# Self attention seven steps earlier, weighted values in three passes, and right factors made from the residual

## The chip, the cores and the metric

The kernel runs on one core of a Trainium2 chip. The metric is the device time of one execution in microseconds (us). Before the change the median of three runs is 722.4 us (722.18 to 723.12). The engines are called as the profile calls them: PE (TensorE, matrix products), DVE (VectorE), ACT (ScalarE), POOL (GpSimd) and SP (SyncE, which only issues transfers).

## The reference

One decoder block on 512 tokens of width 1024, in float32: gated mix of a causal pooling branch and a causal differential attention (4 heads), then cross attention to 256 memory tokens (4 heads), then a squared-ReLU MLP of width 4096, each behind an RMS norm, with residual adds, and a last RMS norm.

```python
h = rms_norm(x, g_mix)
u, q, k, v, gate_logits = split(h @ w_in)
q = apply_rope(q); k = apply_rope(k)
o = diff_attention(q, k, v, lam)     # softmax(q0 k0) - lam * softmax(q1 k1), times v, causal
y_attn = rms_norm(o, g_subln) * (1.0 - lam_init)
mixed = concat([y_pool, y_attn]) * sigmoid(gate_logits)
x = x + mixed @ w_out
x = x + memory_cross_attention(rms_norm(x, g_cross), rms_norm(mem, g_mem), w_cq, w_ckv, w_co)
x = x + square(relu(rms_norm(x, g_mlp) @ w_up)) @ w_down
return rms_norm(x, g_final)
```

## The kernel before

Everything is kept transposed: a tile holds 128 features by 512 tokens. Each float32 operand is split into a high half (`hi`, cast to fp32r by ACT, line 111) and a low half (`lo`, the difference, made by DVE, line 112), and a product is three matmuls: hi·hi, hi·lo, lo·hi (lines 105 to 107). Weights come as blocks of 128x1024; SP issues their load, ACT casts `whi`, DVE makes `wlo`, two projections ahead of their use, with three buffers of each. The split of a product's result into halves is what the next product waits for.

PE's order is written out by hand: it runs its instructions exactly as the program issues them. The orders of the other engines come from a scheduler, which takes the instructions by their dependencies and priority; `tc.high_priority()` raises the priority of what is issued inside. `tile_mm` (a projection of one 128-feature tile) runs over eight k-tiles of its input; each k-tile is a *step* of three matmuls, after which a counter ticks. `after(n, fn)` puts `fn` n steps later, so attention work is dropped between the steps of the projections.

The projections of the first stage run in the order of `PLAN`: `k0 q0 q1 k1 q2 q3 ...`, where g is a gate, u an input of the pooling branch. `qk_proj` makes a rotated q or k: after the matmuls, ACT copies the product into a quarter-swapped tile in four pieces (line 417), DVE multiplies by the cosine (418), POOL by the sine and adds (419, 420), ACT casts the two high halves (423, 425) and DVE makes the two low halves (424, 426). For k, SP copies the result into a partner-swapped tile z by two transfers (430, 431). So the tile `s` of a head holds high and low halves of both components in one array.

Twenty steps (`START`) after q0 the first attention block is due, and one more each six steps (`SPACE`): `scores(h, i)` for head h and block i of 128 queries. For each of two components c it makes two matmuls into a PSUM tile `sc` of three buffers (442, 443); DVE adds the mask and takes the maximum (445), ACT exponentiates (447); then DVE inverts the sums (449, 450), ACT scales one component (451) and DVE combines the two (452). 15 steps (`SOFTMAX`) after the scores `flip(h, i)` transposes the result on PE (463) and splits it into `at` hi and lo. Three steps after a head's last flip `attend(h)` multiplies by v into the tile `av`, over four key blocks of 512, 384, 256 and 128 columns: per block v hi times `at` hi (105), v hi times `at` lo (106), v lo times `at` hi (107). Six steps later `finish` normalises with a sum over features on PE.

In the cross attention, `cross_scores(h)` makes two `sc` tiles (in each, two query blocks), and DVE takes the maxima (684), ACT exponentiates (688), DVE normalises (692); `cross_transpose(h)` transposes and splits into `at`, and `cross_out(h)` multiplies by the memory values and splits into `xg`. The end of this stage is written as: `cross_out(0)`, `cross_scores(3)`, `cross_transpose(2)`, `cross_out(1)`, `cross_out(2)`, then the transpose and output of head 3 inside the following projection ("co").

The MLP's up projection is a Strassen-like product of 256x256 token halves A and B: left factors are sums of weight blocks, right factors sums of the weighted residual `x` (features m and m+4, halves A and B). `done_co(m)` adds the residual (line 572), makes the factors (`right_factors`, 764 to 776; the last two m at high priority) and adds the square to `ss2` (260, 261). For m below 4, x is written as a float32 tile by ACT, x(B) is replaced by the difference, and both are split in one 512-wide cast and subtraction into B11 and T1. For m of 4 and more x is written, then T2 and T3 (into `y`), then B21, B22 and T4 (`right_rest`, 790). The first MLP block (A11) uses B11 of k = 0 to 3 in that order; 11 steps after the last "co" tile PE sums `ss2` over features (234, 235).

Of the kernel before, what the change touches and what calls it, by code (L numbers as in the profile page):

```python
# [13 lines left out]
AF = mybir.ActivationFunctionType  # L14
ALU = mybir.AluOpType
AX = mybir.AxisListType

P = 128
T = 512
D = 1024  # L20
KC = D // P
NT = T // P
M = 256
# [5 lines left out]
LAM_INIT = 0.8 - 0.6 * math.exp(-0.3 * 0)  # L29
WINDOWS = (2, 4, 8, 16)  # L30
PAD = 16
START, SPACE, SOFTMAX, ATTEND, FINISH, POOLING = 20, 6, 15, 3, 6, 23
MEMIN, EARLY, LATE = 16, [4, 5, 6, 0, 1], [2, 7, 3]
WARM = 8
ON_POOL = (1, 3, 5, 7), (1, 3, 5)
# [2 lines left out]
PARTS = "A11", "A12", "A21", "A22"  # L38
ORDER = "A11", "A12", "s1", "s2", "s3", "A22", "s4"
FIRST_ORDER = "A11", "s1", "A12", "s2", "s3", "A22", "s4"  # L40
PLAN = "k0 q0 q1 k1 q2 q3 g4 k2 g5 g6 k3 g7 u0 u1 u2 u3 g0 g1 g2 g3"

G_MIX, G_CROSS, G_MEM, G_MLP, G_FINAL, PSCALE, GSUB, LAMS = 0, 8, 16, 24, 32, 40, 44, 45
NG_COL = LAMS
# [6 lines left out]
def block_kernel(ctx: ExitStack, tc: tile.TileContext, x0g, xT, memT, wv, wm, wst, wckv, wpool, vecs, csts, outT):  # L51
    nc = tc.nc
# [27 lines left out]
    def tmp(dt=F32):  # L80
        return sb("tmp", [P, T], 10, dt)
# [22 lines left out]
    def mm3(o, lh, ll, rh, rl, start, stop):  # L104
        nc.tensor.matmul(o, lh, rh, start=start, stop=False)  # L105
        nc.tensor.matmul(o, lh, rl, start=False, stop=False)  # L106
        nc.tensor.matmul(o, ll, rh, start=False, stop=stop)  # L107


    def split(hi, lo, src, eng=V):  # L110
        S.copy(hi, src)  # L111
        eng.tensor_tensor(lo, src, f(hi), op=ALU.subtract)  # L112
# [150 lines left out]
    def scaled(hi, lo, src, g):  # L263
        S.activation(hi, src, AF.Copy, scale=g)
        V.scalar_tensor_tensor(lo, src, g, f(hi), op0=ALU.mult, op1=ALU.subtract)
# [24 lines left out]
    def tile_mm(o, w, rhs, ks=range(KC), first=True, last=True):  # L290
        ks = list(ks)
        for n, k in enumerate(ks):
            c = slice(k * P, (k + 1) * P)
            mm3(o, w[0][:, c], w[1][:, c], rhs[k][0], rhs[k][1],
                first and n == 0, last and n == len(ks) - 1)
            tick()
# [31 lines left out]
    def W(*key):  # L328
        return weights(where[key])
# [82 lines left out]
    def qk_proj(which, h):  # L412
        o = acc()
        tile_mm(o, W(which, h), xg)
        a, b = tmp(), tmp()
        for j in range(4):
            S.copy(b[32 * (j ^ 1):32 * (j ^ 1) + 32, :], o[32 * j:32 * j + 32, :])  # L417
        V.tensor_tensor(a, o, cos_r, op=ALU.mult)
        ROPE_E.tensor_tensor(b, b, sin_r, op=ALU.mult)
        nc.gpsimd.tensor_tensor(a, a, b, op=ALU.add)  # L420
        s = pair("s", 6)
        top, bot = slice(0, 64), slice(64, 128)
        S.copy(s[top, 0, :], a[top, :])
        V.tensor_tensor(s[bot, 0, :], a[top, :], f(s[top, 0, :]), op=ALU.subtract)
        S.copy(s[bot, 1, :], a[bot, :])
        V.tensor_tensor(s[top, 1, :], a[bot, :], f(s[bot, 1, :]), op=ALU.subtract)
        st[which, h] = s
        if which == "k":
            z = pair("s", 6)
            nc.sync.dma_start(f(z[top, :, :]), f(s[bot, :, :]))  # L430
            nc.sync.dma_start(f(z[bot, :, :]), f(s[top, :, :]))
            st["z", h] = z
# [36 lines left out]
    def attend(h):  # L469
        at = st["at", h]  # L470
        o = ps("av", 1)
        e = slice(h * P, (h + 1) * P)
        for b in range(NT):
            vh, vl = st["v"][b]
            mm3(o[:, b * P:], vh[:, e], vl[:, e], at[0][:, b, b * P:], at[1][:, b, b * P:],
                b == 0, b == NT - 1)
        sq = tmp()
        S.activation(sq, o, AF.Square)
        sp = split_sq(sq, T)

        def finish():
            s = ps("tr", 2)
            bcast_sum(s, *sp)
            y = tmp()
            rsqrt(y, s, 1.0 / P, sq, tmp(),
                  lambda r: V.scalar_tensor_tensor(r, o, st["gsub"], r, op0=ALU.mult, op1=ALU.mult))
            merge(4 + h, y)

        after(FINISH, finish)
# [183 lines left out]
    def cross_scores(h):  # L673
        es = []
        for j in range(NT // 2):
            o = ps("sc", 3)
            for b in range(2):
                i = 2 * j + b
                tb = slice(i * P, (i + 1) * P)
                for c in range(2):  # L680
                    q, k = st["cq", 2 * h + c], st["mk", 2 * h + c]
                    mm3(o[:, b * M:(b + 1) * M], q[0][:, tb], q[1][:, tb], k[0], k[1], c == 0, c == 1)
            mx, sm = small(2), small(2)
            V.tensor_reduce(mx, o.rearrange("p (b m) -> p b m", b=2), axis=AX.X, op=ALU.max, negate=True)
            e = tmp()
            for b in range(2):
                c = slice(b * M, (b + 1) * M)
                S.activation(e[:, c], o[:, c], AF.Exp, bias=mx[:, b:b + 1], accum_out=sm[:, b:b + 1])
            V.reciprocal(sm, sm)
            for b in range(2):  # L690
                c = slice(b * M, (b + 1) * M)
                V.tensor_scalar(e[:, c], e[:, c], sm[:, b:b + 1], None, op0=ALU.mult)
            es.append(e)
        st["p", h] = es

    def cross_transpose(h):
        t = sb("at", [P, NT, T], 2, F32R)
        pt = (t[:, :MT, :], t[:, MT:, :])
        for j, e in enumerate(st["p", h]):
            tr = ps("tr", 2)  # L700
            for c in range(MT):
                for b in range(2):
                    nc.tensor.transpose(tr[:, (2 * c + b) * P:(2 * c + b + 1) * P],
                                        e[:, b * M + c * P:b * M + (c + 1) * P], ident)
            src = tr.rearrange("p (c t) -> p c t", c=MT)
            split(pt[0][:, :, j * M:(j + 1) * M], pt[1][:, :, j * M:(j + 1) * M], src)
        st["pt", h] = pt

    def cross_out(h):
        pt = st["pt", h]  # L710
        for dc in range(2):
            o = acc()
            m = 2 * h + dc
            c = slice((m % 4) * P, (m % 4) * P + P)
            for i in range(MT):
                vh, vl = st["mv", m // 4, i]
                mm3(o, vh[:, c], vl[:, c], pt[0][:, i, :], pt[1][:, i, :], i == 0, i == MT - 1)
            pr = pair("xg", 8)
            split(pr[:, 0, :], pr[:, 1, :], o)
            cross_o[m] = (pr[:, 0, :], pr[:, 1, :])  # L720
# [16 lines left out]
            after(2, cross_transpose, m // 2 - 1)  # L737
    flush()
    cross_out(0)
    cross_scores(3)  # L740
    cross_transpose(2)
    cross_out(1)
    cross_out(2)
    after(2, cross_transpose, 3)
# [11 lines left out]
    def right_factors(m, t):  # L756

        k = m % 4
        g = vec[:, G_MLP + m:G_MLP + m + 1]
        x = tmp()  # L760
        pr = pair("mix", 8)
        if m < 4:
            b12 = tmp()[:, :M]
            S.activation(x[:, A], t[:, A], AF.Copy, scale=g)
            S.activation(b12, t[:, B], AF.Copy, scale=g)
            V.tensor_tensor(x[:, B], x[:, A], b12, op=ALU.subtract)
            xs[k] = (x[:, B], b12)
            split(pr[:, 0, :], pr[:, 1, :], x)
            parts("B11", k, pr[:, 0, :], pr[:, 1, :], A)
            parts("T1", k, pr[:, 0, :], pr[:, 1, :], B)  # L770
            return
        S.activation(x, t, AF.Copy, scale=g)
        t1, b12 = xs[k]
        y = tmp()
        V.scalar_tensor_tensor(y[:, A], x[:, B], -1.0, t1, op0=ALU.mult, op1=ALU.subtract)
        V.tensor_tensor(y[:, B], x[:, B], b12, op=ALU.subtract)
        p2 = pair("s", 6)
        split(p2[:, 0, :], p2[:, 1, :], y)
        parts("T2", k, p2[:, 0, :], p2[:, 1, :], A)
        parts("T3", k, p2[:, 0, :], p2[:, 1, :], B)  # L780
        parts("B21", k, pr[:, 0, :], pr[:, 1, :], A)
        parts("B22", k, pr[:, 0, :], pr[:, 1, :], B)
        if m < KC - 1:
            right_rest(k, x, y, pr)
        else:
            rest.append((k, x, y, pr))

    def right_rest(k, x, y, pr):
        split(pr[:, 0, :], pr[:, 1, :], x)
        V.scalar_tensor_tensor(y[:, A], y[:, A], -1.0, x[:, A], op0=ALU.mult, op1=ALU.subtract)  # L790
        if k % 2 == 0:
            half["T4"] = pair("s", 6)
        c = slice(k % 2 * M, k % 2 * M + M)
        split(half["T4"][:, 0, c], half["T4"][:, 1, c], y[:, A])
        parts("T4", k, half["T4"][:, 0, :], half["T4"][:, 1, :], c)
# [10 lines left out]
    def renew():  # L806
# [2 lines left out]
        early.close()  # L809
        late["pool"] = ctx.enter_context(tc.tile_pool(name="late", bufs=1))  # L810

    projection("co", cross_o, [0, 1, 2, 3, 4, 5], [6, 7], done_co, renew, CO_ORDER)
    with tc.high_priority():
        sp2 = split_sq(ss2, T)
# [215 lines left out]
```

## Time and profile before

| | before |
|---|---|
| median of 3 runs | 722.4 us (722.18 to 723.12) |
| the profiled execution's own time | 722.57 us |
| its span, first to last instruction | 720.8 us |
| mean granted TensorE clock | 0.998 |
| busy share PE / DVE / ACT / POOL | 98% / 71% / 54% / 9% |
| DMA | 91.09 MB, mean 126 GB/s |

A row of the timeline gives the start in us, the duration, the engine, the line, the operation, output<-input and the count; in brackets stand the idle time ahead of it and what ended it. Several equal instructions in a row are one row with a count. Ends of matmuls are modelled, so neighbours overlap in the rows: a matmul of 512 columns starts 0.23 us after the last one and is shown with 0.39. A row of the window view gives a stretch and, for PE, weight loads, DVE, ACT and POOL, busy time and instructions, then granted clock, DMA share and GB/s.

### The profile page before, as it was taken

Reading aid. Unit: us, or ns where it says so; the run is one execution under the profiler, and the core shown is the slowest. Engines: PE = TensorE matmul, PEld = TensorE weight load, DVE = VectorE, ACT = ScalarE, POOL = GpSimd, SP = SyncE. Lnnn points to the kernel's source line nnn. Section 1 sums busy time; section 2 is a strip of 40 time slices with the busy share of each in tenths; the row PEclk is TensorE's granted clock in tenths of the full one; section 3 lists DMA queues with packets and bytes.
Section 4 is the critical chain, followed back from the end, with each engine's and each line's share of the span. In section 5 each row is a group of like instructions: output and inputs, shape, how many; then the busy total and the mean of one; then the engine's idle time right before and its main releaser. Section 6 shows DMA issues by size and latency. Waiting matters only on the chain.

```text
span 720.8 us, 10378 instructions
## 1 busy us (share of the span) xinstructions
PE 706.5 (98%) x4016; PEld 617.0 (86%) x4016; DVE 510.6 (71%) x797; ACT 392.5 (54%) x646; POOL 66.9 (9%) x59
## 2 busy tenths in 40 slices
PE   8999999999999999999999999999999999999995
PEld 6887888788889888888879988999889988899894
DVE  7698999975888546572999954598446973589525
ACT  7498998676766434452865641355214641256432
POOL 0044112534000000000000000000000000000000
PEclk9999999999999999999999999999999999999999
DMA  8443223143525552113924850558216661305103
GB/s 315 151 118 116 88 75 116 60 146 119 176 88 176 181 170 83 65 58 143 246 79 127 237 164 30 150 111 294 89 33 167 205 182 58 88 30 161 45 1 116
DMA packets 28257, 91.09 MB, mean 126 GB/s; under 512 B 3089, under 2 KB 5137, under 8 KB 28209
## 3 DMA queue, kind: packets, MB, share of 16 engines
q1 hardware_dynamic: 25856, 81.92, 33.5%
q0 software_dynamic: 2352, 8.52, 7.0%
q8 instruction: 31, 0.51, 0.3%
q14 instruction: 18, 0.14, 0.1%
HBM read 86.24 MB, written 2.10 MB: 123 GB/s over the span
## 4 chain that ended last, share of the span: by engine, by line
PE 89%; DVE 5%; ACT 4%; issue 1%; DMA 0%; POOL 0%; DVEq 0%; SPq 0%; ACTq 0%
PE acc L105 17%; PE acc L106 17%; PE acc L107 17%; PE sc L105 11%; PE sc L106 11%; PE sc L107 11%; ACT tmp L447 1%; PE sc L386 1%; PE sc L388 1%; PE sc L390 1%; DVE tmp L445 1%; DVE wlo L112 1%; ACT tmp L417 1%; ACT whi L111 1%; DMA wraw<-wv 0%
## 5 line engine op out<-in xcount | busy, mean ns | idle before, releaser
L111 ACT CAST whi<-wraw 128x1024 fp32r<-128x1024 f32 (+1 forms) x94 | 97.2, 1035 | 107.5 <-PE acc L106 41.0
L105 PE MATMUL acc<-xg,whi 128*128 128x512 f32 x392 | 155.0, 395 | 0.0
L107 PE MATMUL acc<-xg,wlo 128*128 128x512 f32 x392 | 153.0, 390 | 0.0
L106 PE MATMUL acc<-xg,whi 128*128 128x512 f32 x392 | 152.7, 390 | 0.0
L112 DVE TENSOR_TENSOR wlo<-wraw,whi 128x1024 fp32r<-128x1024 f32 (+1 forms) x94 | 115.1, 1226 | 26.8 <-ACT whi L111 26.4
L107 PEld LDWEIGHTS acc<-xg,wlo 128*128 128x128 f32 x392 | 73.6, 188 | 15.8
L105 PEld LDWEIGHTS acc<-xg,whi 128*128 128x128 f32 x392 | 73.7, 188 | 14.5
L106 PEld LDWEIGHTS acc<-xg,whi 128*128 128x128 f32 x392 | 73.7, 188 | 14.3
L572 DVE TENSOR_TENSOR vr<-acc,vr 128x512 f32<-128x512 f32 x39 | 26.9, 690 | 76.5 <-PE acc L107 76.4
L105 PE MATMUL sc<-mix,whi 128*128 128x256 f32 (+1 forms) x184 | 54.2, 295 | 0.0
L107 PE MATMUL sc<-mix,wlo 128*128 128x256 f32 (+1 forms) x184 | 54.1, 294 | 0.0
L106 PE MATMUL sc<-mix,whi 128*128 128x256 f32 (+1 forms) x184 | 54.0, 294 | 0.0
L164 POOL DMA_DIRECT2D mraw<-wst x16 | 13.8, 864 | 429.1 <-DMA mraw<-wst 302.3
L111 ACT CAST whi<-mraw 128x1024 fp32r<-128x1024 f32 x24 | 25.0, 1052 | 45.9 <-PE acc L106 33.0
L890 DVE TENSOR_TENSOR tmp<-sc,tmp 128x512 f32<-128x512 f32 x56 | 37.5, 684 | 6.5 <-PE sc L107 6.4
L111 ACT CAST mhl<-wraw 128x1024 fp32r<-128x1024 f32 x19 | 20.0, 1052 | 34.4 <-PE acc L106 18.0
L106 PE MATMUL acc<-xg,mhl 128*128 128x512 f32 x96 | 37.4, 390 | 0.0
L105 PE MATMUL acc<-xg,mhl 128*128 128x512 f32 x96 | 37.4, 389 | 0.0
L107 PE MATMUL acc<-xg,mhl 128*128 128x512 f32 x96 | 37.4, 389 | 0.0
L107 PEld LDWEIGHTS sc<-mix,wlo 128*128 128x128 f32 x184 | 34.5, 188 | 1.1
L105 PEld LDWEIGHTS sc<-mix,whi 128*128 128x128 f32 x184 | 34.6, 188 | 1.0
L106 PEld LDWEIGHTS sc<-mix,whi 128*128 128x128 f32 x184 | 34.5, 187 | 1.1
(274 smaller groups left out, 1731.4 us busy)
## 6 DMA issues: line engine op xcount, KB each, us to landing
wraw<-wm SPq DMA_DIRECT2D x76, 512.0 KB, 3.5
mraw<-wst SPq DMA_DIRECT2D x24, 512.0 KB, 3.9
wraw<-wckv SPq DMA_DIRECT2D x16, 512.0 KB, 3.4
mraw<-wst POOLq DMA_DIRECT2D x16, 512.0 KB, 6.1
wraw<-wst SPq DMA_DIRECT2D x16, 512.0 KB, 3.4
s<-s SPq DMA_DIRECT2D x8, 256.0 KB, 3.7
vr<-xT SPq DMA_DIRECT2D x8, 256.0 KB, 4.5
outT<-mix SPq DMA_DIRECT2D x8, 256.0 KB, 2.4
```

The lines of the kernel that those rows point to most:

```text
L105: nc.tensor.matmul(o, lh, rh, start=start, stop=False)
L106: nc.tensor.matmul(o, lh, rl, start=False, stop=False)
L107: nc.tensor.matmul(o, ll, rh, start=False, stop=stop)
L111: S.copy(hi, src)
L112: eng.tensor_tensor(lo, src, f(hi), op=ALU.subtract)
L164: nc.gpsimd.dma_start(r, part(n, then), accum_op=ALU.add)
L386: nc.tensor.matmul(o[i], xg[k][0][:, tb], wh[:, c], start=k == 0, stop=False)
L388: nc.tensor.matmul(o[i], xg[k][1][:, tb], wh[:, c], start=False, stop=False)
L390: nc.tensor.matmul(o[i], xg[k][0][:, tb], wl[:, c], start=False, stop=k == KC - 1)
L417: S.copy(b[32 * (j ^ 1):32 * (j ^ 1) + 32, :], o[32 * j:32 * j + 32, :])
L572: V.tensor_tensor(t, o, t, op=ALU.add)
L890: V.tensor_tensor(u[new], o, u[old], op=ALU.add)
```

## The change

There are five parts. `START` is 13 instead of 20 and the gates g4 and g6 stand behind k2 and k3 in `PLAN`. The rotation of q and k is a function of its own, at high priority for head 0. `attend` runs over the four key blocks in three passes instead of block by block. `cross_transpose(2)` stands ahead of `cross_scores(3)`. And `right_factors` makes all factors from the residual tile `t` with the weight g, or its negative in the small tile `ng`, inside the DVE instruction, so that the copy x is not written for m of 4 and more, and for m below 4 the halves A and B are split apart.

```diff
-START, SPACE, SOFTMAX, ATTEND, FINISH, POOLING = 20, 6, 15, 3, 6, 23
+START, SPACE, SOFTMAX, ATTEND, FINISH, POOLING = 13, 6, 15, 3, 6, 23
-PLAN = "k0 q0 q1 k1 q2 q3 g4 k2 g5 g6 k3 g7 u0 u1 u2 u3 g0 g1 g2 g3"
+PLAN = "k0 q0 q1 k1 q2 q3 k2 g4 g5 k3 g6 g7 u0 u1 u2 u3 g0 g1 g2 g3"
@@ qk_proj
         tile_mm(o, W(which, h), xg)
+        with tc.high_priority() if h == 0 else nullcontext():
+            rotate(which, h, o)
+
+    def rotate(which, h, o):
         a, b = tmp(), tmp()
...
@@ attend
-        for b in range(NT):
-            vh, vl = st["v"][b]
-            mm3(o[:, b * P:], vh[:, e], vl[:, e], at[0][:, b, b * P:], at[1][:, b, b * P:],
-                b == 0, b == NT - 1)
+        for v, a in ((0, 0), (1, 0), (0, 1)):
+            for b in range(NT):
+                nc.tensor.matmul(o[:, b * P:], st["v"][b][v][:, e], at[a][:, b, b * P:],
+                                 start=v + a + b == 0, stop=a == 1 and b == NT - 1)
@@ cross attention
     cross_out(0)
+    cross_transpose(2)
     cross_scores(3)
-    cross_transpose(2)
     cross_out(1)
@@ right_factors
-        g = vec[:, G_MLP + m:G_MLP + m + 1]
-        x = tmp()
+        g, ng = vec[:, G_MLP + m:G_MLP + m + 1], st["ng"][:, m:m + 1]
         pr = pair("mix", 8)
         if m < 4:
-            b12 = tmp()[:, :M]
-            S.activation(x[:, A], t[:, A], AF.Copy, scale=g)
+            scaled(pr[:, 0, A], pr[:, 1, A], t[:, A], g)
+            x = tmp()
+            t1, b12 = x[:, A], x[:, B]
             S.activation(b12, t[:, B], AF.Copy, scale=g)
-            V.tensor_tensor(x[:, B], x[:, A], b12, op=ALU.subtract)
-            xs[k] = (x[:, B], b12)
-            split(pr[:, 0, :], pr[:, 1, :], x)
+            V.scalar_tensor_tensor(t1, t[:, A], g, b12, op0=ALU.mult, op1=ALU.subtract)
+            xs[k] = (t1, b12)
+            split(pr[:, 0, B], pr[:, 1, B], t1)
...
-        S.activation(x, t, AF.Copy, scale=g)
         t1, b12 = xs[k]
         y = tmp()
-        V.scalar_tensor_tensor(y[:, A], x[:, B], -1.0, t1, op0=ALU.mult, op1=ALU.subtract)
-        V.tensor_tensor(y[:, B], x[:, B], b12, op=ALU.subtract)
+        V.scalar_tensor_tensor(y[:, A], t[:, B], ng, t1, op0=ALU.mult, op1=ALU.subtract)
+        V.scalar_tensor_tensor(y[:, B], t[:, B], g, b12, op0=ALU.mult, op1=ALU.subtract)
...
-    def right_rest(k, x, y, pr):
-        split(pr[:, 0, :], pr[:, 1, :], x)
-        V.scalar_tensor_tensor(y[:, A], y[:, A], -1.0, x[:, A], op0=ALU.mult, op1=ALU.subtract)
+    def right_rest(k, t, g, ng, y, pr):
+        scaled(pr[:, 0, :], pr[:, 1, :], t, g)
+        V.scalar_tensor_tensor(y[:, A], t[:, A], ng, y[:, A], op0=ALU.mult, op1=ALU.subtract)
...
+    st["ng"] = home[:, 568:568 + KC]
+    V.tensor_scalar(st["ng"], vec[:, G_MLP:G_MLP + KC], -1.0, None, op0=ALU.mult)
```

`scaled(hi, lo, src, g)`, which was there before, is an ACT copy with scale g into `hi` (line 264) and one DVE instruction src·g − hi into `lo` (265).

On PE, the rows around scores(0,0) before. `acc_541` is the projection q2, `s_395` is k0, `s_400` its swapped copy z0, `s_443` is q0, and the two `sc` tiles are the two components:

```order
L107 MATMUL acc_541<-xg_172,wlo_452 128x512
L105 MATMUL acc_541<-xg_190,whi_451 128x512
L106 MATMUL acc_541<-xg_190,whi_451 128x512
L107 MATMUL acc_541<-xg_190,wlo_452 128x512
L442 MATMUL sc_561<-s_395,s_443 128x128
L443 MATMUL sc_561<-s_400,s_443 128x128
L442 MATMUL sc_568<-s_395,s_443 128x128
L443 MATMUL sc_568<-s_400,s_443 128x128
L105 MATMUL acc_541<-xg_214,whi_451 128x512
```

And after; `acc_493` is the projection k1, which comes ahead of q2:

```order
L106 MATMUL acc_493<-xg_214,whi_406 128x512
L107 MATMUL acc_493<-xg_214,wlo_407 128x512
L446 MATMUL sc_516<-s_395,s_443 128x128
L447 MATMUL sc_516<-s_400,s_443 128x128
L446 MATMUL sc_523<-s_395,s_443 128x128
L447 MATMUL sc_523<-s_400,s_443 128x128
L105 MATMUL acc_493<-xg_232,whi_406 128x512
L106 MATMUL acc_493<-xg_232,whi_406 128x512
```

The four matmuls moved from the fourth step of q2 to behind the fifth step of k1, seven steps earlier. From here on, four is added to the line numbers.

On DVE, the rows that make k0's and q0's low halves, before (`acc_448` is q1's product):

```order
L426 TENSOR_TENSOR s_395<-tmp_386,s_395 64x512
L112 TENSOR_TENSOR wlo_497<-wraw_449,whi_496 128x1024
L418 TENSOR_TENSOR tmp_479<-acc_448,cst_68 128x512
L424 TENSOR_TENSOR s_443<-tmp_434,s_443 64x512
L426 TENSOR_TENSOR s_443<-tmp_434,s_443 64x512
L112 TENSOR_TENSOR wlo_545<-wraw_494,whi_544 128x1024
L418 TENSOR_TENSOR tmp_524<-acc_493,cst_68 128x512
```

and after:

```order
L430 TENSOR_TENSOR s_395<-tmp_386,s_395 64x512
L112 TENSOR_TENSOR wlo_497<-wraw_449,whi_496 128x1024
L422 TENSOR_TENSOR tmp_479<-acc_448,cst_68 128x512
L428 TENSOR_TENSOR s_443<-tmp_434,s_443 64x512
L430 TENSOR_TENSOR s_443<-tmp_434,s_443 64x512
L449 ISA tmp_519,small_520<-sc_516,cst_68 128x128
L449 ISA small_520 128x1
L449 ISA tmp_526,small_527<-sc_523,cst_68 128x128
```

Up to q0's second low half the order is the same; behind it the maxima of scores(0,0) took the place of the next weight's low half and of k1's product. It is the same on ACT: the order is unchanged up to q0's casts, and then the exponential of scores(0,0) stands ahead of the weight cast.

On DVE after the change, ahead of scores(3,2) (`acc_1315` is the projection u1, `sc_1332` the first component of scores(3,1), whose PSUM buffer scores(3,2) takes next):

```order
L112 TENSOR_TENSOR at_1175<-tr_1359,at_1174 128x4x128
L536 TENSOR_TENSOR padu_1372<-acc_1315,rstd_315 128x512
L535 MEMSET padu_1499 128x16
L112 TENSOR_TENSOR wlo_1393<-wraw_1316,whi_1392 128x1024
L449 ISA tmp_1335,small_1336<-sc_1332,cst_68 128x256
```

The maximum of scores(3,1) stands behind the low half of a flip, u1's product and a weight's low half.

On DVE after the change, at the start of the MLP, from behind the residual of m = 7 (`vr_1901`) and one addition of a square, to the low half of the sum of squares (`tmp_3650`), which PE asks for 11 steps into the MLP:

```order
L793 SCALAR_TENSOR_TENSOR tmp_3543<-vr_1899,vx_67,tmp_3543 128x256
L112 TENSOR_TENSOR wlo_3672<-mraw_3559,whi_3671 128x1024
L112 TENSOR_TENSOR mix_3591<-tmp_3594,mix_3591 128x256
L778 SCALAR_TENSOR_TENSOR tmp_3635<-vr_1901,vx_67,tmp_3594 128x256
L779 SCALAR_TENSOR_TENSOR tmp_3635<-vr_1901,vx_67,tmp_3594 128x256
L265 SCALAR_TENSOR_TENSOR mix_3634<-vr_1901,vx_67,mix_3634 128x512
L261 TENSOR_TENSOR ss_3247<-ss_3247,tmp_3641 128x512
L179 TENSOR_TENSOR mraw_3559<-mraw_3559,wraw_3603 128x1024
L112 TENSOR_TENSOR mhl_3709<-wraw_3662,mhl_3708 128x1024
L112 TENSOR_TENSOR s_3552<-tmp_3543,s_3552 128x256
L112 TENSOR_TENSOR s_3638<-tmp_3635,s_3638 128x512
L112 TENSOR_TENSOR tmp_3650<-ss_3247,tmp_3649 128x512
```

Before, this stretch had the 512-wide split of factor 3 (`mix`) behind the weight's low half; now that factor's half A is made ahead of the stretch, and two 256-wide pieces (half B's and T4's of the m before) stand in it.

More of the change, by code (lines that the diff above doesn't have):

```diff
@@ L783, in right_factors @@
         if m < KC - 1:
-            right_rest(k, x, y, pr)
+            right_rest(k, t, g, ng, y, pr)
         else:
-            rest.append((k, x, y, pr))
-    def right_rest(k, x, y, pr):
-        split(pr[:, 0, :], pr[:, 1, :], x)
-        V.scalar_tensor_tensor(y[:, A], y[:, A], -1.0, x[:, A], op0=ALU.mult, op1=ALU.subtract)
+            rest.append((k, t, g, ng, y, pr))
+    def right_rest(k, t, g, ng, y, pr):
+        scaled(pr[:, 0, :], pr[:, 1, :], t, g)
+        V.scalar_tensor_tensor(y[:, A], t[:, A], ng, y[:, A], op0=ALU.mult, op1=ALU.subtract)
         if k % 2 == 0:
```

## The prediction

> **What bounds the kernel now.** I read the page's busy shares and chain first, then TensorE's waits, then the timeline around each wait.
>
> ```profile
> span 720.8 us, 10378 instructions
> PE 706.5 (98%) x4016; PEld 617.0 (86%) x4016; DVE 510.6 (71%) x797; ACT 392.5 (54%) x646; POOL 66.9 (9%) x59
> PE sc L106 <- DVE mix L112: 1.0, 1, 1.0
> PE sc L442 <- DVE small L445: 0.9, 2, 0.7
> PE av L106 <- DVE at L112: 0.7, 2, 0.4
> PE tr L463 <- DVE tmp L452: 0.3, 1, 0.3
> ```
>
> The last four rows say what TensorE (PE) waited for longest inside the kernel: total, times, longest. Its order is fixed by hand and it is 98% busy, so the time is its matmuls plus its waits. The change removes no matmul, so the question is how much waiting goes and how much comes. The ends of matmuls are modelled, so a wait is better read from starts: the next matmul usually starts 0.23 us after one of 512 columns, 0.17 after 384, 0.12 after 256. What exceeds this is the loss, and 0.1 more where the matmul behind the wait is itself that much longer than its like (0.50 for 0.39 in the rows below).
>
> The other engines' average shares mislead: in the attention stage there is no slack.
>
> ```profile
> 80.00:100.00 20.00, 19.59 (x97) 16.11 (x96) 17.61 (x44) 19.76 (x45) 2.58 (x2) 1.00 0.31 93
> 120.00:140.00 20.00, 19.05 (x93) 15.61 (x92) 19.10 (x54) 12.07 (x28) 10.09 (x8) 1.00 0.25 80
> ```
>
> The columns after the window are its length, then the busy time of PE, PE's weight loads, DVE, ACT and POOL. ACT is busy 19.76 of 20 us at 80 to 100 us, DVE 19.10 at 120 to 140. Whatever PE asks for sooner here must wait for a queue that is full.
>
> **What the change removes.** First the attention waits of before, as pairs of starts on PE.
>
> ```profile
> 69.95 0.39 PE L107 MATMUL acc<-xg,wlo 128*128 128x512 f32 x1
> 70.66 0.41 PE L463 MATMUL tr<-cst,tmp 128*128 128x128 f32 x2 [0.32 <-DVE tmp L452]
> 83.69 0.48 PE L105 MATMUL av<-at,vr 128*128 128x512 f32 x1
> 84.58 0.50 PE L106 MATMUL av<-at,vr 128*128 128x512 f32 x1 [0.41 <-DVE at L112]
> 107.02 0.40 PE L105 MATMUL av<-at,vr 128*128 128x512 f32 x1
> 107.73 0.50 PE L106 MATMUL av<-at,vr 128*128 128x512 f32 x1 [0.32 <-DVE at L112]
> 130.11 0.34 PE L443 MATMUL sc<-s,s 128*128 128x384 f32 x1
> 131.19 0.44 PE L442 MATMUL sc<-s,s 128*128 128x384 f32 x1 [0.75 <-DVE small L445]
> ```
>
> They lose 0.71 − 0.23 = 0.48 at flip(0,1), 0.89 − 0.23 + 0.11 = 0.77 and 0.71 − 0.23 + 0.11 = 0.59 at the attends of heads 0 and 1, and 1.08 − 0.17 + 0.10 = 1.01 at scores(3,2). The smaller one of the two on line 442, worked out in the same way, is 0.46. **Attention total: 3.31 us.** The new pass order asks for the low half of `at` only after both passes over the high half, seven matmuls of 128 to 512 columns and about 0.95 us later, more than the 0.66 and 0.48 of waiting proper, so I cost 0.77 and 0.59 as gone.
>
> **What it adds first: a wait at scores(0,0).** START 13 puts it seven k-steps earlier on PE. A step is three matmuls, 0.68 us, so 4.76 us.
>
> ```profile
> 53.03 0.22 PE L442 MATMUL sc<-s,s 128*128 128x128 f32 x1
> 45.92 2.35 ACT L417 COPY tmp<-acc 32x512 f32<-32x512 f32 x4
> 48.30 0.62 ACT L423 CAST s<-tmp 64x512 fp32r<-64x512 f32 x1
> 48.30 0.69 DVE L418 TENSOR_TENSOR tmp<-acc,cst 128x512 f32<-128x512 f32 x1
> 49.02 1.16 DVE L424 TENSOR_TENSOR s<-tmp,s 64x512 fp32r<-64x512 f32 x1
> 50.22 1.68 DVE L426 TENSOR_TENSOR s<-tmp,s 64x512 fp32r<-64x512 f32 x1
> 47.14 0.46 SPq L431 DMA_DIRECT2D s<-s  x1
> s<-s SPq DMA_DIRECT2D x8, 256.0 KB, 3.7
> ```
>
> PE reaches it at 53.03 − 4.76 = 48.27. It needs q0 entire. ACT casts q0's high halves from 48.30, after q1's four copies (2.35); DVE makes the low halves behind q1's product, and the second ends at 50.22 + 1.68 = 51.90. The order of both queues up to there is the same after the change: the priority given to q0's rotation moved nothing ahead of q1's copies and product. All these rows wait for earlier work, none for PE's scores, so their times should hold. The swapped copy of k0, issued at 47.14, lands about 3.7 later, 50.84, inside the same wait. So PE, which would go on at 48.43 with the second half of the pair (c1), goes on at about 52.0: **+3.6 us**, firm to a few tenths. Before, the same data had a margin of 53.03 − 51.90 = 1.1. Behind it on PE stand the last three steps of k1, so k1's copies on ACT come as late as PE. ACT and DVE do not use all of the wait: ACT's next row is now the exponential of scores(0,0), which stands ahead of the next weight cast and k1's copies, and waits until about 52.3.
>
> **What it adds in the rest of attention.** From there everything follows PE at the same step distance as before, but ACT starts the softmax chain with less done. Durations for the walk:
>
> ```profile
> 56.39 1.04 ACT L111 CAST whi<-wraw 128x1024 fp32r<-128x1024 f32 x1
> 64.43 0.60 ACT L447 ACTIVATE tmp<-tmp,small 128x384 f32<-128x384 f32 x1
> 70.08 0.61 ACT L451 ACTIVATE tmp<-tmp,small 128x384 f32<-128x384 f32 x1
> 73.32 0.61 DVE L452 SCALAR_TENSOR_TENSOR tmp<-tmp,small,tmp 128x384 f32<-128x384 f32 x1
> ```
>
> *flip(0,2).* PE asks 27 steps after the scores: 52.0 + 27 × 0.69 + about 2.9 of scores and transposes between = 73.6. Its softmax on ACT stands behind, in the new order: three sets of four copies (2.35 each, 7.1), three pairs of casts (1.28 a pair, 3.8), three weight casts (2.9), eight exponentials with their accumulator reads (0.5 to 0.7 each, 4.8), two scalings and a transposed cast (1.0), and its own scaling (0.6): 20.2. From 52.3 that is 72.5; rows that wait at the head of the queue for PE or DVE I put at 1.6, an estimate from walking the two queues (0.8 to 1.9), so 74.1. DVE adds 0.61: 74.7. **+1.1** (0.3 to 1.4).
>
> *Small ones.* At scores(0,3) and flip(0,3) I find 0.2 and 0.1 the same way.
>
> *scores(3,2).* Its c1 takes the PSUM buffer that the maximum of scores(3,1) must release. In the new DVE order u1's product and a weight's low half stand just ahead of that maximum.
>
> ```profile
> 125.46 2.06 DVE L112 TENSOR_TENSOR wlo<-wraw,whi 128x1024 fp32r<-128x1024 f32 x1
> 130.71 0.41 DVE L445 CUSTOM_DVE_ANT_0 tmp<-sc,cst 128x256 f32<-128x256 f32 x1
> 131.05 0.68 DVE L532 TENSOR_TENSOR padu<-acc,rstd 128x512 f32<-128x512 f32 x1
> ```
>
> After u1's last matmul DVE needs 0.68 + 1.2 to 2.06 + 0.41 = 2.3 to 3.15 less 0.1 to 0.2 of overlap, and PE asks about 1.0 after that matmul's end. The wait is 1.2 to 2.0, with `at`(2,3)'s low half ahead up to 2.4; I take 1.9, near the row of 2.06, since POOL also works there (10.09 of 20). Sum after: 3.6 + 1.1 + 0.3 + 1.9 = 6.9, less 3.31: **+3.6** (from +0.3, if the first wait makes all later ones go, to +4.5). The gate that moves behind k2 and k3 moves no matmul in or out, and k2's swapped copy keeps its six steps to scores(2,0).
>
> **Cross attention and MLP.**
>
> ```profile
> 322.11 0.40 PE L107 MATMUL acc<-at,mix 128*128 128x512 f32 x1
> 322.92 0.50 PE L105 MATMUL acc<-at,mix 128*128 128x512 f32 x1 [0.41 <-DVE xg L112]
> 374.04 0.28 PE L107 MATMUL sc<-mix,mhl 128*128 128x256 f32 x1
> 374.69 0.39 PE L105 MATMUL sc<-mix,mhl 128*128 128x256 f32 x1 [0.37 <-ACT mix L111]
> 376.03 0.39 PE L106 MATMUL sc<-mix,mhl 128*128 128x256 f32 x1 [0.96 <-DVE mix L112]
> 373.30 0.69 DVE L572 TENSOR_TENSOR vr<-acc,vr 128x512 f32<-128x512 f32 x1 [0.65 <-PE acc L107]
> 382.96 0.39 PE L235 MATMUL tr<-tmp,ones 128*128 128x512 f32 x1
> ```
>
> *Cross:* transposing head 2 before scoring head 3 lets its casts start sooner but ends scores(3) 0.8 later, and the `xg` split still comes behind that softmax on DVE. Of the 0.81 − 0.23 + 0.11 = 0.69 lost at 322.92 I take **−0.1** (0 to −0.69).
>
> *MLP:* 376.03 − 374.04 − 2 × 0.12 + 0.11 = 1.86 is lost at 374.69 and 376.03, where the first block asks for right factor 3. It now has its high half on ACT ahead of a weight cast that waits for PE, and its low half on DVE ahead of m=7's residual: **−1.86 there**. But DVE's work between that residual (373.30) and the sum of squares that PE asks for 11 steps into the MLP hardly shrinks: in the new order 0.61 + 0.60 + 0.34 + 1.14 + 3 × 0.34 + 0.66 + 0.60 + 2 × 1.14 + 0.34 + 0.60 + 0.68 = 8.87, ending at 382.17. PE, no longer held up, asks at 382.96 − 1.86 = 381.10: a new wait of about **+1.1**, and 0 to 0.3 behind it. Net **−0.5** (0 to −1.86). The removed ACT copies (four of 0.6 to 0.7) lie on an engine that waits for PE there, and the one added small DVE operation of −g in DVE's idle time: nothing.
>
> **Sum.** +3.6 − 0.1 − 0.5 = +3.0 on the profiled execution, whose own time is 722.57 (span 720.8 and 1.8 around it), 0.17 above the median of 722.4. I forecast **725.4 us**.
>
> **Rivals.** *No change:* the first wait lets ACT and DVE catch up, and the later attention waits vanish: 3.6 − 3.31 − 0.6 = −0.3, so 722.3. For it: 3.6 us more for two full queues. Against: ACT stands still for 2.7 of them behind the first exponential. *Faster:* q0's rotation does come first. If its casts ran ahead of q1's copies (2.35), its second low half would end near 49.5, the first wait would be 1.2, and with the later ones gone the time 722.57 + 1.2 − 3.31 − 0.6 = 719.9. It decides once the first wait is under about 2.3 and the later ones are gone. Against: the queue order shows the casts behind those copies. *Slower still:* a gap of this length lowers PE's clock.
>
> ```profile
> L127 PE MATMUL acc<-tmp x8: 380/634/634, 1.2 to 4.0; 128*128 128x512 bf16 x8
> ```
>
> The only matmuls that follow a long idle time are those of the start, 634 ns instead of 380 for some 2.5 us, a loss of 2.5 × (1 − 380/634) = 1.0; once or twice that again is 726.4 to 727.4. Against: no wait of before inside the kernel (up to 1.3) is followed by slow matmuls, and q0's wait is broken into pieces by the first half's two matmuls at about 50.2 and 50.9. [...]
>
> **How the numbers follow.** Forecast 0.60 (723.9 to 726.9 for the bounds of the later waits), no change 0.17, faster 0.08, clock drop 0.07, and 0.08 for the DVE waits at their upper bounds, 727 or more. Within 0.2% (±1.4 us, about what a measurement of this kernel can tell from no change) lies the second alone: slower 0.75, same 0.17, faster 0.08. The range leaves out the fastest case and the tails: 721.9 to 727.4.
>
> **What would show it.** Right: PE rows of scores(0,0) at 48 to 52 waiting for DVE's `s`; ACT idle until 52; a wait of `tr` near 75 for DVE and of `sc` near 128 for the maximum; none at `av`; the first MLP block without a wait, and one at the sum of squares near 384. Wrong: q0's low halves before 50, or TensorE's later attention waits together under 1 us.

## The result

| | before | after |
|---|---|---|
| median of four executions | 722.4 us (722.18 to 723.12) | 732.62 us (731.63 to 733.74) |
| ratio, 95% interval | | 1.0136 [1.0123, 1.0149] |
| the profiled execution's own time, span | 722.57, 720.8 us | 733.74, 731.9 us |
| mean granted TensorE clock | 0.998 | 0.992 |
| busy share PE / DVE / ACT / POOL | 98 / 71 / 54 / 9% | 97 / 70 / 53 / 9% |

The change makes the kernel 10.2 us slower. The forecast was 725.4 (721.9 to 727.4): the direction holds, the size does not. In the profiled executions the difference is 11.2 us, since the profiled one of the changed kernel is the slowest of its four.

The page of the changed kernel, its busy shares and its chain by engine:

```profile
PE 711.8 (97%) x4016; PEld 619.4 (85%) x4016; DVE 512.5 (70%) x802; ACT 388.5 (53%) x642; POOL 68.7 (9%) x59
PE 79%; DVE 11%; ACT 6%; issue 3%; DMA 1%; DVEq 0%; SPq 0%; ACTq 0%
```

PE runs the same 4016 matmuls and shows 5.3 us more of them, so some ran slower. In the chain that ended last PE falls from 89% to 79%, and DVE rises from 5% to 11%. PE's waits in the changed kernel (total, times, longest; line numbers are four higher than before):

```profile
PE sc L446 <- DVE small L449: 2.0, 1, 2.0
PE sc L446 <- DVE s L428: 1.8, 1, 1.8
PE tr L467 <- DVE tmp L456: 1.4, 2, 1.2
PE tr L235 <- DVE tmp L112: 1.3, 2, 1.1
PE sc L446 <- DVE s L430: 1.2, 1, 1.2
PE acc L105 <- DVE xg L112: 0.5, 1, 0.5
PE tr L105 <- DVE at L112: 0.5, 1, 0.5
PE acc L106 <- DVE xg L112: 0.2, 1, 0.2
```

The two waits at `av` and those at the first MLP block have gone from the list. New are the waits for q0's two low halves (L428, L430) and for the sum of squares (L235); longer are the one for the maximum of scores(3,1) (L449) and those of the flips for the combined softmax result (L456). The place with the most loss, on PE's timeline:

```profile
47.95 0.39 PE L107 MATMUL acc<-xg,wlo 128*128 128x512 f32 x1
50.12 0.33 PE L446 MATMUL sc<-s,s 128*128 128x128 f32 x1 [1.78 <-DVE s L428]
50.28 0.27 PE L447 MATMUL sc<-s,s 128*128 128x128 f32 x1
51.79 0.48 PE L446 MATMUL sc<-s,s 128*128 128x128 f32 x1 [1.24 <-DVE s L430]
52.06 0.42 PE L447 MATMUL sc<-s,s 128*128 128x128 f32 x1
52.28 0.73 PE L105 MATMUL acc<-xg,whi 128*128 128x512 f32 x1
52.81 0.63 PE L106 MATMUL acc<-xg,whi 128*128 128x512 f32 x1
...
55.30 0.40 PE L106 MATMUL acc<-xg,whi 128*128 128x512 f32 x1
55.53 0.39 PE L107 MATMUL acc<-xg,wlo 128*128 128x512 f32 x1
```

PE stands from 48.2 to 51.79, as forecast (48.27 to 52.0): 2.17 − 0.23 = 1.94, then 1.51 − 0.11 = 1.40, so 3.3 us. What follows was only a rival in the forecast: the projection's matmuls take 0.63 instead of 0.39, and their starts are 0.43 instead of 0.23 apart. The next window view of the changed kernel shows why, around this place and a second one like it at scores(3,2): after the length come the busy times of PE, weight loads, DVE, ACT and POOL, and third from the end the granted clock.

```profile
48.37:51.78 3.41, 0.44 (x2) 0.30 (x2) 3.32 (x4) 1.07 (x2) 2.74 (x2) 1.00 0.68 211
51.78:55.19 3.41, 3.40 (x9) 2.82 (x10) 2.28 (x8) 2.11 (x6) 0.00 (x0) 0.50 0.02 5
130.29:133.70 3.41, 1.40 (x9) 1.05 (x8) 2.67 (x8) 1.80 (x6) 2.58 (x2) 1.00 0.14 19
133.70:137.11 3.41, 3.41 (x13) 3.03 (x13) 2.62 (x10) 0.95 (x3) 1.75 (x2) 0.50 0.36 139
```

The clock is granted at half for exactly 3.41 us, twice, each time behind 3.41 us in which PE was idle for more than half of the time. Each is worth up to 3.41 × 0.5 = 1.7 us, and by the starts of PE's matmuls each did cost 1.7: from the second `sc` pair to 55.9 us 3.1 us are lost, of which the wait is 1.4, and from 132.7 to 137.4 us 3.9, of which the wait is 2.2.

### The profile page after: what moved, and what is told of

It is laid out like the page before. It is cut to its first block, busy times and chain, and to the rows that moved or that the text cites. A ratio compares the mean times of both kernels' runs of the same rounds, so it can differ in the third digit from the quotient of the medians.

```text
span 731.9 us, 10383 instructions
## 1 busy us (share of the span) xinstructions
PE 711.8 (97%) x4016; PEld 619.4 (85%) x4016; DVE 512.5 (70%) x802; ACT 388.5 (53%) x642; POOL 68.7 (9%) x59
## 4 chain that ended last, share of the span: by engine, by line
PE 79%; DVE 11%; ACT 6%; issue 3%; DMA 1%; DVEq 0%; SPq 0%; ACTq 0%
PE acc L105 15%; PE acc L106 15%; PE acc L107 15%; PE sc L105 9%; PE sc L107 9%; PE sc L106 9%; DVE wlo L112 2%; ACT tmp L421 2%; DMA wraw<-wm 1%; DVE tmp L895 1%; ACT whi L111 1%; PE sc L386 1%; PE av L479 1%; PE sc L388 1%; PE sc L390 1%
## 5 line engine op out<-in xcount | busy, mean ns | idle before, releaser
L112 DVE TENSOR_TENSOR wlo<-wraw,whi 128x1024 fp32r<-128x1024 f32 (+1 forms) x94 | 116.7, 1243 | 28.1 <-ACT whi L111 27.8
```

## The experiments

The theory at this point: (a) START 13 asks for data that its queues have not made, which costs waits; (b) such waits bring the half clock, and so cost more than their length; (c) the rest of the change is worth little. The rival is that the order of the gates, the passes or the right factors cause the later waits. One thing needed no run: without the priority for head 0's rotation the instruction order of every engine is the same, row for row, so that part does nothing.

### START back to 20

```diff
-START, SPACE, SOFTMAX, ATTEND, FINISH, POOLING = 13, 6, 15, 3, 6, 23
+START, SPACE, SOFTMAX, ATTEND, FINISH, POOLING = 20, 6, 15, 3, 6, 23
```

> The changed kernel with START back at 20 and everything else of the change kept. Theory (the lost time comes from asking seven steps too early): the wait at scores(0,0) (3.6 us in the changed kernel's rows), the half clock behind it (3.4 us at 0.5, so 1.7 us) and the waits at flip(0,2) and flip(0,3) (1.9 us) go, about 7 us, and if the wait at scores(3,2) with its half clock (2.3 and 1.7 us) goes too, 11: 721 to 726 us. Rival (the new order of the gates, the priority of head 0's rotation or the pass order put the work of DVE and ACT in a worse order): the waits after 60 us stay, 728 us or more.

Measured: 726.74 us (726.71 to 727.02), 1.0057 [1.0042, 1.0073] of before. That is above the theory's 726 and under the rival's 728. The wait at scores(0,0) and both half clocks are gone, and 5.9 us with them; but 4 us stay, which is neither theory. Its trace has new or longer waits: 1.4 at flip(0,3), 0.9 at `av` of head 1 (0.5 before), 1.3 at a flip at 112 us, and 2.0 at the scores of head 3 (1.3 before).

### Only the order of the gates, and everything but START and that order

On the kernel before, and on the kernel with START 20, with opposite signs:

```diff
-PLAN = "k0 q0 q1 k1 q2 q3 g4 k2 g5 g6 k3 g7 u0 u1 u2 u3 g0 g1 g2 g3"
+PLAN = "k0 q0 q1 k1 q2 q3 k2 g4 g5 k3 g6 g7 u0 u1 u2 u3 g0 g1 g2 g3"
```

> The kernel before with only the new order of the gates, k2 and k3. Theory (the order alone costs, whatever the pass order: k2's four copies and two casts reach ACT a tile earlier, amid the softmaxes of heads 0 and 1): 3 to 4.5 us slower, 725.5 to 727. Rival (it costs only together with the three passes): within 1 us of the kernel before.

> The changed kernel with START back at 20 and the old order of the gates too, so that passes, the cross stage's order and the right factors are what is left of the change. Theory (with the gates behind k2 and k3, the rotations of k2 and k3 fall among the softmaxes of heads 0 and 1, and the waits at 80.0, 108.6 and 112.2 us of the START 20 kernel, 3.5 us together, come from there): about 723 us. Rival (the pass order has moved them): 726 us or more, as with START 20 alone.

Measured: the new order alone 726.88 us, 1.0054 [1.0034, 1.0074]; START 20 with the old order and all other parts 722.88, 1.0002 [0.9992, 1.0011]. Both as the theory said. With START 20 the order of the gates costs the whole 4 us, and passes, cross order and right factors together are worth nothing that can be told from zero. One place where it costs, on ACT in the START 20 kernel, while head 0's last scores wait for their exponential, and then on DVE, where their two halves are combined (L456) for flip(0,3):

```profile
71.93 1.17 ACT L421 COPY tmp<-acc 32x512 f32<-32x512 f32 x2
73.00 0.61 ACT L427 CAST s<-tmp 64x512 fp32r<-64x512 f32 x1
73.64 0.62 ACT L429 CAST s<-tmp 64x512 fp32r<-64x512 f32 x1
74.28 1.17 ACT L421 COPY tmp<-acc 32x512 f32<-32x512 f32 x2
75.48 0.72 ACT L451 ACTIVATE tmp<-tmp,small 128x512 f32<-128x512 f32 x1
79.21 1.21 DVE L112 TENSOR_TENSOR wlo<-wraw,whi 128x1024 fp32r<-128x1024 f32 x1
80.76 0.73 DVE L456 SCALAR_TENSOR_TENSOR tmp<-tmp,small,tmp 128x512 f32<-128x512 f32 x1
```

k2's copies (L421) come a tile sooner, ahead of the exponential at 75.48; PE asks for flip(0,3) at 80.27 and gets it at 81.64. ACT is only a part of it: its scaling of this block (L455) ends 0.87 us ahead of PE's request, for 1.72 with the old order, and DVE then combines the halves only at 80.76, behind a gate and a weight's low half. That the earlier k2 causes this wait, through both queues, is read from them and was not tried by itself.

### START 13 with the old order, without and with the other parts

> The kernel before with only START 13. Theory (START alone makes the loss; passes, cross order and right factors are worth nothing together, as START 20 with the old order of the gates showed): the 3.4 us at scores(0,0), the low halves of q0 ending near 51.8 us, and a total near that of START 13 with the old order and the other parts, 734 to 738 us. A half clock behind the first wait or not, as the 3.41 us windows fall. Rival (the three passes spare START 13 waits that the block order brings, two at 0.5 to 0.8 us each): 737.5 us or more.

> The changed kernel with the old order of the gates, START 13 kept. The start of the stage is the same (the two orders differ only from the seventh tile on), so the wait of 3.4 us at scores(0,0) and the half clock behind it stay in both theories, 5.1 us. Theory (two causes that add: the early start, 5.9 us between START 13 and 20, and the order of the gates, 3.9 us at START 20): 722.9 + 5.9 = 728.8, 727 to 730. Rival (the order of the gates costs only with START 20, where it meets other work): 732 us or more.

Measured: START 13 alone on the kernel before 735.71 us, 1.0166 [1.0139, 1.0194]; all of the change but the order of the gates 736.11, 1.0182 [1.0166, 1.0197]. START 13 alone was within its range (its rival, 737.5 or more, falls), and again the other parts are worth nothing that can be told from zero. The two causes do not add: the sum 728.8 is far off, and the rival of the second kernel holds. Its first wait is as long as expected, but no half clock follows it; one follows a wait at 75 us instead (last section). With START 13 the new order saves 3.5 us (736.11 to 732.62), with START 20 it costs 3.9. The waits view of START 13 with the old order and the other parts shows what the new order saves:

```profile
PE sc L446 <- DVE small L449: 2.8, 1, 2.8
PE tr L467 <- DVE tmp L456: 2.6, 2, 2.4
PE sc L446 <- DVE s L428: 1.8, 1, 1.8
PE sc L447 <- DMA s<-s: 1.4, 2, 0.8
```

Two waits for k's swapped copies (DMA, L447) that the changed kernel has not, and longer ones at the flips and at the scores of head 3: with the early start k2 and k3 themselves are late unless they are computed sooner.

### START 16

```diff
-START, SPACE, SOFTMAX, ATTEND, FINISH, POOLING = 13, 6, 15, 3, 6, 23
+START, SPACE, SOFTMAX, ATTEND, FINISH, POOLING = 16, 6, 15, 3, 6, 23
```

> The changed kernel with START 16. PE asks for scores(0,0) three steps (2.04 us) later than with 13. Theory (the wait is the distance to the end of q0's second low half, and the clock falls only after a gap of some 2 us or more): a wait of 1.5 to 1.7 us there and no half clock at 52 to 55 us. Rival (any wait over 1.3 us brings the half clock): the same wait, followed by 3.4 us at half clock. The time is between 726.7 (START 20) and 732.6 (START 13).

Measured: 735.28 us (732.73 to 736.8), 1.0167 [1.0144, 1.0190], above the range given. The first wait is right: one of 1.4 us, with no half clock behind it. The median is above that of START 13, but the two intervals overlap, and the profiled execution, 732.73, is the fastest of its four. So what the runs show is that three steps of distance give nothing back, not that they cost more. The gain at the first wait is taken by others:

```profile
PE av L479 <- DVE at L112: 5.1, 3, 2.4
PE tr L235 <- DVE tmp L112: 3.1, 2, 2.0
PE sc L446 <- DVE s L430: 1.2, 1, 1.2
```

5.1 us for the low halves of `at` at three attends, where the changed kernel loses 0.2 and START 20 waits for 0.8. Behind one of them, of 2.5 us, the clock is at half from 134.9 to 138.4 us. DVE's rows stand in another order than with START 13, and with the order the places change at which DVE is late. The distance between a request and its data, which explains the first wait, does not explain these.

### Filling the waits with matmuls

14 extra matmuls ahead of scores(0,0), and in the second kernel 8 more ahead of scores(3,2); what they write is overwritten by the scores.

```diff
             o = ps("sc", 3)
+            for _ in range({(0, 0, 0): 14, (3, 2, 0): 8}.get((h, i, c), 0)):
+                nc.tensor.matmul(o, xg[0][0][:, :P], xg[0][0], start=True, stop=True)
             nc.tensor.matmul(o[:, :n], q[:, c, tb], k[:, c, :n], start=True, stop=False)
```

> The changed kernel with 14 extra matmuls of 512 columns (3.2 us, results unused) ahead of scores(0,0), which keep TensorE at work while it would wait. Theory (the clock falls because TensorE stands still): no row of half clock at 52 to 55 us, 1.7 us less there; if ACT sets the pace of the softmax chain behind it, up to that much comes back as a longer wait at flip(0,2) (1.4 us in the changed kernel): 731 to 732.6 us. If the chain has room, 730.9. Rival (the clock falls for another reason, such as the changing load): the half clock stays, 732.6 us.

> The same with 8 more extra matmuls (1.8 us) ahead of scores(3,2), whose second component waits 2.0 us in the changed kernel. Theory: no half clock at 133.8 to 137.2 us either, and nothing behind it in the attention is as tight as at flip(0,2), so 1.0 to 1.7 us less than with the first filling alone. Rival: the half clock stays, or the waits at 142 to 166 us (1.7 us together) take all of it back: the same time as with the first filling.

Measured: 731.27 us with one filling (1.0119 [1.0105, 1.0133]), 730.92 with two (1.0117 [1.0103, 1.0131]). The first filling, in the window view of its kernel:

```profile
47.77:51.18 3.41, 3.41 (x17) 2.83 (x16) 3.35 (x4) 2.32 (x4) 2.15 (x2) 1.00 0.85 217
51.18:54.59 3.41, 3.24 (x17) 2.66 (x16) 3.18 (x6) 1.73 (x4) 0.76 (x1) 1.00 0.16 58
129.69:133.10 3.41, 1.41 (x9) 1.10 (x8) 2.59 (x9) 1.72 (x6) 2.70 (x2) 1.00 0.13 37
133.10:136.51 3.41, 3.41 (x13) 3.03 (x12) 2.69 (x12) 1.02 (x2) 1.62 (x2) 0.50 0.31 121
```

Work that does nothing but keep PE busy removes the half clock at 52 us and leaves the one at 133. That PE's standing still brought the first one is shown: with the filling PE is busy for 3.41 and 3.24 us of the two stretches that hold the wait. It is worth 1.35 us by the medians (730.79 to 731.83 for 731.63 to 733.74), as the theory said (0 to 1.7). In the traces the stretch around it becomes 1.5 us shorter: of the 5.1 us lost between 40 and 60 us 0.4 are left, and the extra matmuls take 3.2. With the second filling the clock stays whole at 133 us too (granted at 1.00 from 128 to 140 us), but the median is only 0.35 us lower, which the ranges do not tell from nothing, against 1.0 to 1.7 expected: waits at 139.6 and 152.9 us, 0.3 and 0.65, stand in its trace and not in that of the first, so a good part was taken back.

### Parts alone

The three passes on the kernel before (diff as in the change):

> The kernel before with only the three passes of the weighted values. Theory: the waits for the low half of at at heads 0 and 1 (0.77 and 0.59 us) go, nothing else moves: 1.0 to 1.4 us faster, about 721.2 us. Rival (the time is taken back at the next wait in a stage in which ACT and DVE are full): within 0.3 us of the kernel before.

Measured: 723.36 us, 1.0006 [0.9993, 1.0018]: the 1.0 to 1.4 us of the theory are excluded, and its rival, within 0.3 us, is not. The waits at `av` go, and those at the scores of head 3 grow from 0.9 to 2.2 us in the view of waits:

```profile
PE sc L442 <- DVE small L445: 2.2, 2, 1.2
```

The right factors alone, and then with the sum of squares asked for one step later (STAT2 12 for 11):

> The kernel before with only the right factors made from the residual. Theory: the 1.86 us lost at the first MLP block go and 1.27 come at the sum of squares, 0.35 at the block behind it: net -0.2 us, within 0.5 us of the kernel before. Rival (the waits at 424 us in the down projection, 0.8 us in the changed kernel and in the one with START 20, belong to this part): 0.6 to 1.0 us slower.

> The kernel before with the right factors made from the residual and the sum of squares asked for 12 steps into the MLP instead of 11 (one step of six matmuls of 256 columns, 0.71 us later). Theory (only the place of the request is wrong; the sum itself is ready at the same time): the wait of 1.27 us shrinks to 0.56 and the time is 0.5 to 0.7 us under that of the right factors alone, 0.4 to 0.7 under the kernel before. Rival (DVE is late as a whole): the rest moves to the next block's buffer, which waits 0.35 now, and the time stays.

Measured: 722.84 us, 1.0002 [0.9991, 1.0012], and 722.93, 1.0004 [0.9995, 1.0013]. The first is as the theory said: 1.86 us go, 1.27 and 0.36 come; its rival falls, for its trace has no wait in the down projection. In the second the rival holds: the wait at the sum falls to 0.58 and the one at the next block grows to 1.13, the sum 1.7 instead of 1.6. DVE as a whole is late at this place.

With one addition of weight blocks moved to POOL, to relieve DVE:

```diff
-            V.tensor_tensor(r, r, raw[n, "A11" if name == "s2" else "A12"], op=ALU.add)
+            (G if (n, name) == (0, "s2") else V).tensor_tensor(
+                r, r, raw[n, "A11" if name == "s2" else "A12"], op=ALU.add)
```

> The kernel before with the right factors made from the residual, and the first addition of weight blocks at the start of the MLP (128x1024, 1.14 us of DVE) made by POOL, which is idle there. Theory (with 12 steps the wait only moved by one block, so DVE is late as a whole at this place, by the 1.6 us that the two waits have together): 1.1 us less of them, 0.5 left, and 721.2 to 722.0 us. Rival (POOL's slower addition holds up the block that needs the sum, or slows DVE's own rows): the waits stay at 1.6 us or grow, 722.6 or more.

Measured: 725.85 us (723.72 to 727.23), 1.0037 [1.0025, 1.0048], slower. POOL takes 2.9 us for what DVE does in 1.2, but that is not what PE waits for: the scheduler now puts a weight's low half ahead of the sum's, and the waits at the sum are 0.9 and 2.2 us in the profiled execution, the fastest of its runs. Why the others are up to 3.5 us slower stays open. No version beats the kernel before.

## Why the prediction was wrong, point by point

Three steps of the prediction failed. It kept the half clock out of its sum, and that measured 3.4 us in the profiled execution. It took the places that it had not walked as free, and they measured 2.5 us. And it put the order of the gates at nothing, though this order is worth 3.9 us one way or 3.5 the other: START 13 alone costs 13.1 us (735.71 for 722.61), and the new order gives 3.5 of them back.

Forecast and measured, in us of the profiled execution, as starts on PE beyond the usual spacing (without the 0.1 behind each wait, which the forecast has in two of its terms):

| place | forecast | measured |
|---|---|---|
| scores(0,0), wait | 3.6 | 3.3 |
| flip(0,2) | 1.1 | 1.36 |
| scores(0,3), flip(0,3) | 0.3 | 0.67 |
| scores(3,2) | 1.9 | 2.17 |
| half clock, twice | not in the sum | 3.4 |
| 141 to 166 us, four waits | none found | 1.7 |
| attention waits of before that go | −3.31 (−2.9 without the 0.1s) | −2.9 |
| cross, xg | −0.1 | +0.07 (0.65 for 0.58) |
| MLP, first block and sum of squares | −0.5 | −0.14 (1.27 + 0.35 for 1.76) |
| down projection at 430 | none | +0.8 |

The last column adds up to 10.4 of the 11.2 us. Of the rest 0.2 is a wait that stays at `av` of head 0, and what is left is spread over many matmuls and was not traced.

**The wait at scores(0,0) is right in cause, place and size.** DVE's rows stood where they stood before: the second low half ended at 51.74, for 51.90.

```profile
48.93 1.13 DVE L428 TENSOR_TENSOR s<-tmp,s 64x512 fp32r<-64x512 f32 x1
50.10 1.64 DVE L430 TENSOR_TENSOR s<-tmp,s 64x512 fp32r<-64x512 f32 x1
52.10 0.40 ACT L451 ACTIVATE tmp<-tmp,small 128x128 f32<-128x128 f32 x1 [2.64 <-DVE small L449]
```

ACT's idle time is there as well, 2.64 for 2.7 (last row). So ACT did not use the first wait to catch up, and the later waits stayed: the no-change rival is refuted. That q0's rotation would come first is refuted too.

**The waits at flip(0,2) and scores(3,2) are right in place, each 0.3 short.** The rows on PE, and on DVE for the second:

```profile
76.88 0.52 PE L467 MATMUL tr<-cst,tmp 128*128 128x128 f32 x3 [1.21 <-DVE tmp L456]
132.67 0.44 PE L446 MATMUL sc<-s,s 128*128 128x384 f32 x1 [2.01 <-DVE small L449]
131.08 1.20 DVE L112 TENSOR_TENSOR wlo<-wraw,whi 128x1024 fp32r<-128x1024 f32 x1
132.20 0.41 DVE L449 CUSTOM_DVE_ANT_0 tmp<-sc,cst 128x256 f32<-128x256 f32 x1
```

The maximum at 132.20 stands behind u1's product and the weight's low half, where the order put it. That low half took 1.20, not the 2.06 that the forecast's 1.9 leaned on, so the size is near by luck in part.

**Wrong: the clock.** "A gap of this length lowers PE's clock" had a chance of 0.07 and stood outside the sum. Two reasons against it were given. "Broken into pieces" was wrong: the two matmuls between, 0.44 us, did not count for enough. That waits up to 1.3 had brought no slow matmuls was true but said nothing of 2 and 3.3. The price, 1.0 to 2.0, was right for one, 1.7; it came twice, the second time behind the wait of 2.17 whose place the same text forecast. This is the largest term missing, 3.4 us by the starts; filling shows 1.35 us of it by the medians.

**Wrong: the sum stopped where the walk stopped.** Four waits at 141 to 166 us, 1.7 in all, and 0.8 in the down projection stood in no term; places that were not walked counted as nothing. The first four are gone with START 20, and three of them stand in the trace of START 13 alone, so they come with the early start; which row of DVE makes them was not traced. The one in the down projection stays with START 20 and is in neither trace of the fillings nor in that of the right factors alone; its cause stays open.

**Mis-sized: what the other parts give back.** The gain by the passes was booked in full (1.36 with restarts) and that of the right factors as 0.5. Alone, neither can be told from nothing ([0.9993, 1.0018] and [0.9991, 1.0012]): their waits came back at the scores of head 3 and at the sum of squares. The latter, 1.1 in the forecast, measured 1.27 and 0.35 behind it.

**Wrong: the order of the gates at nothing.** The reason given, "moves no matmul in or out", is true and not enough. With START 13 the new order saves 3.5 us, with START 20 it costs 3.9. By the rows above, which were read and not tried, it moves the time at which ACT and DVE get k2's work and at which the swapped copies of k2 and k3 land, not what PE computes.

## What to carry to other kernels

Here a request that was moved ahead of its data cost the gap, 3.3 us at scores(0,0), and in two of the three kernels of the last section more, 5.1 and 6.3 us, where half clock came with it: price both, for waits as long as those that brought it here (2.0 us and more in the changed kernel), and try filling to tell them apart. With ACT and DVE full, waits that a part removed came back elsewhere: the passes took away those at `av` (0.77 and 0.59 us by the starts), and those at the scores of head 3 grew from 0.9 to 2.2; the right factors took away 1.86 us at the first MLP block, and 1.27 and 0.36 came at the sum of squares and behind it. So a wait that a part removes is not yet time gained: run the part alone. A scheduler orders the engines here, and the parts did not add: the order of the gates cost 3.9 us with START 20 and saved 3.5 with START 13. In such a kernel run the set too, and trust no sum.

## What the runs showed of the hardware

In the changed kernel the granted clock is at half from 51.78 and from 133.70 us, for 3.41 us each. The two begin 24.0 times 3.41 us apart, the first of them 15.2 times 3.41 us behind the kernel's first instruction; in the kernel with one filling the drop at 133.10 is 39.0 times 3.41 us behind it. So the stretches of 3.41 us below are counted from the drops of their own execution, not from its start. In these traces half clock set in behind stretches with little work on PE, and the length of a wait alone does not tell where. With START 13 and the old order of the gates, the same 3.3 us wait straddles two stretches; the view of that kernel:

```profile
46.90:50.32 3.42, 1.85 (x9) 1.19 (x7) 3.36 (x4) 2.90 (x5) 1.57 (x2) 1.00 0.85 182
50.32:53.73 3.41, 1.96 (x10) 1.60 (x11) 2.58 (x7) 1.19 (x4) 1.28 (x1) 1.00 0.33 130
74.21:77.62 3.41, 1.05 (x7) 0.73 (x6) 3.41 (x11) 3.38 (x11) 2.03 (x2) 1.00 0.00 0
77.62:81.03 3.41, 3.41 (x11) 2.68 (x10) 2.06 (x5) 3.12 (x7) 0.00 (x0) 0.51 0.45 154
```

Busy 1.85 and 1.96 of 3.41, and no drop; busy 1.05 at 74 us, and half clock in the stretch that follows. The other stretches at full clock that half clock followed had PE busy for 0.44 and 1.40 us (changed kernel), 1.41 (one filling), 1.33 (START 16) and about 1.3 (START 13 alone, by its rows on PE). Counted in the same way up to the last matmul, the trace of the kernel before (from its drop at 717.21, behind its last matmul) has 207 stretches, with 2.24 us and more, and that of the changed kernel 206 besides its four, with 2.21 and more; none of these was followed by half clock. START 16 has one with 1.69 us, and the clock stayed at 1.00 behind it. Its rows, and then the first wait of the kernel before with START 13 alone:

```profile
131.56:134.97 3.41, 1.33 (x7) 1.20 (x8) 3.41 (x14) 1.08 (x3) 0.27 (x1) 1.00 0.48 154
134.97:138.38 3.41, 3.41 (x10) 2.55 (x9) 1.76 (x5) 1.92 (x7) 1.28 (x1) 0.50 0.02 5
141.79:145.20 3.41, 1.69 (x7) 1.43 (x8) 3.41 (x5) 0.00 (x0) 2.49 (x2) 1.00 0.47 154
51.60:55.02 3.42, 2.46 (x7) 2.08 (x8) 2.58 (x7) 2.10 (x6) 0.35 (x1) 0.50 0.07 26
55.02:58.43 3.41, 3.41 (x10) 2.64 (x9) 1.12 (x4) 1.57 (x3) 0.00 (x0) 0.50 0.00 0
```

In the latter 1.0 us of the wait lay inside the stretch at half clock, and a second one followed, behind 2.46 us of busy PE at half clock (from 51.60 to 58.43 in all). So one wait of 3.3 us cost 3.6, 5.1 or 6.3 us beyond the usual spacing between 40 and 60 us in these three kernels, as the stretches fell. The executions of one kernel differ in the granted clock too: the changed kernel took 731.63 us with a mean of 0.995 and 733.74 with 0.992, START 16 732.73 with 0.994 and 735.24 to 736.8 with 0.989 to 0.993; only one of each was traced, so where the half clock fell in the others is not shown. PE's busy time was varied by filling alone, at two places; how little work keeps the clock whole is not shown.
